# First FFN matrix as seven quarter products, with the residual stream and the inner features passed through DRAM

## The chip, the cores and the metric

The kernel runs on one core of a Trainium2 chip. The metric is the device time of one execution in microseconds. The engines are TensorE (PE; its weight loads are shown as PEld), VectorE (DVE), ScalarE (ACT), GpSimd (POOL) and SyncE (SP), which here only issues DMA. Each engine takes its own instructions in order; semaphores make one wait for another.

## The reference

One step of a decoder layer (depth 1, width 2048) on 512 prompt tokens and 8 sample tokens: modulated norm, one input projection into sliding-window attention and an RWKV-7 mixer, output projection, gated residual; then the FFN, which is what the change touches:

```python
h2 = _modulate(_rmsnorm(x, g_norm_ffn[l]), sh2, sc2)
gate, up = jnp.split(h2 @ w_ffn_in[l], 2, axis=-1)      # 2048 -> 2 x 5632
x = x + gt2[:, None, :] * ((jax.nn.silu(gate) * up) @ w_ffn_out[l])   # 5632 -> 2048
y = _rmsnorm(x, g_norm_final)
```

## The kernel before

Activations are stored feature by partition: 16 blocks of 128 features, and the 520 tokens as two halves of `HB` = 260 columns (256 of the prompt, 4 of the samples). The residual `x1` stays in SBUF from the output projection to the end.

Matrix products run on float32r halves: a value is cast to a high part, and the rest is a low part (`split`, L143 and L144). `unit` (L81) loads 128x512 of a weight by SP into `raw` (3 buffers), ACT casts `wh` (L88), DVE subtracts to `wl` (L91), each with 3 buffers. `mm3` (L94) then issues, for each 128x128 weight block, three products (high by high, high by low, low by high) for each column half. `main_tile` forms one output tile of 128 features: 16 blocks x 3 x 2 = 96 matmuls into two PSUM banks.

`wout_half` ends the output projection one column half after the other, so that half 0 is normed (`norm_half`, a background generator stepped by `pump` with rough costs in `PacedCore`) while half 1 still multiplies. It does this in weight units that serve 12 matmuls. `accumulate` and `accumulate_half` (L1167, L1178) add a PSUM tile, times the gate, to the residual.

`ffn_phase` follows. `first_pair` runs half 0 of the first gate and up tile while half 1 is normed. Then there are 11 blocks of 4 feature tiles: for each feature tile a gate tile and an up tile (`main_tile`), Silu on ACT (L1417), the product on DVE (L1421), the split into `gH`, `gL`. After the first tile of a block, `out_block` multiplies the block before by its rows of the second matrix, 16 output tiles of 24 matmuls, each accumulated in `x1`. `last_block` ends by halves, with the final norm and the writes.

The tile framework fixes each engine's order when the program is built: it takes the instructions by the order of the program, and sets one behind others where its operands or buffers are not free yet by its own reckoning. It adds the semaphores.

## Time and profile before

| | |
|---|---|
| median of 3 runs | 2761.9 us (2759.91 to 2763.59) |
| the profiled execution, its own time | 2761.62 us |
| its span, first to last instruction | 2759.8 us |
| mean granted TensorE clock | 0.982 |
| busy: PE, DVE, ACT, POOL | 2679.3, 1356.5, 923.4, 223.6 us |
| HBM read, written | 332.86 MB, 18.55 MB |

Times are in microseconds from the span's start. In a group of instructions "x352" is the count; then come busy time, mean nanoseconds of one, and the idle time of the engine ahead of them with what ended it. A busy PE is not the same as a PE at its peak, since matmuls overlap: the step from one to the next is read from a stretch of time and the count in it.

### The profile page before, as it was taken

The numbers are of one execution on the slowest core, as the hardware profiler recorded it, in microseconds if no ns is written. First come the engines' busy times: TensorE is split into PE (matmuls) and PEld (weight loads), VectorE is DVE, ScalarE is ACT, GpSimd is POOL, SyncE is SP. The second block draws the span as 40 slices with busy tenths as digits, with TensorE's granted clock in tenths as the row PEclk, the third lists the DMA queues.
The fourth block names the chain that finished last, engine by engine and source line by source line (L and its number), as shares of the span: only waits on it lengthen the run. The fifth ranks groups of instructions, "written<-read, shape, count | busy, mean of one in ns | idle before, by whom it ended". The sixth has DMA issues, their size and how long they took to land.

```text
span 2759.8 us, 58911 instructions
## 1 busy us (share of the span) xinstructions
PE 2679.3 (97%) x24461; PEld 2479.0 (90%) x24461; DVE 1356.5 (49%) x3266; ACT 923.4 (33%) x1816; POOL 223.6 (8%) x300
## 2 busy tenths in 40 slices
PE   7899999999999999989999999999999999999998
PEld 5577777887787898979999999999999999999997
DVE  2465677767755465682434343434343434343436
ACT  3133445455432344552222222222222222222225
POOL 1012122222111000130000000000000000000004
PEclk9899999999989999999999999999999999999999
DMA  8865554555556732322222222222222222222223
GB/s 296 308 200 149 153 152 141 161 150 151 175 163 206 255 133 100 113 80 92 91 93 90 93 92 93 92 92 93 92 93 92 92 93 92 93 92 93 90 96 110
DMA packets 189900, 354.25 MB, mean 128 GB/s; under 512 B 27665, under 2 KB 38849, under 8 KB 189345
## 3 DMA queue, kind: packets, MB, share of 16 engines
q1 hardware_dynamic: 185584, 339.30, 37.1%
q0 software_dynamic: 3408, 10.15, 1.2%
q8 instruction: 191, 3.13, 0.5%
q10 hardware_dynamic: 640, 1.05, 0.1%
q14 instruction: 77, 0.62, 0.1%
HBM read 332.86 MB, written 18.55 MB: 127 GB/s over the span
## 4 chain that ended last, share of the span: by engine, by line
PE 59%; DVE 2%; DMA 1%; ACT 1%; POOL 0%; issue 0%; DVEq 0%; SPq 0%; ACTq 0%; POOLq 0%
PE pm L98 36%; PE pf L98 18%; PE po L98 3%; PE pl L49 1%; PE pO L49 0%; PE pt L49 0%; PE psc L49 0%; DVE wl L91 0%; DVE x L1178 0%; DMA raw<-in_w_fi 0%; DVE h2L L49 0%; DVE u L49 0%; ACT h2H L49 0%; DMA raw<-in_w_out 0%; POOL u L49 0%
## 5 line engine op out<-in xcount | busy, mean ns | idle before, releaser
L88 ACT CAST wh<-raw 128x512 fp32r<-128x512 f32 (+2 forms) x751 | 460.9, 615 | 1266.8 <-PE pm L98 807.1
L91 DVE TENSOR_TENSOR wl<-raw,wh 128x512 fp32r<-128x512 f32 (+2 forms) x751 | 522.3, 697 | 690.2 <-ACT wh L88 688.8
L98 PE MATMUL pm<-h2H,wh 128*128 128x260 f32 x2816 | 571.2, 282 | 2.2 <-ACT wh L88 1.2
L98 PE MATMUL pm<-h2L,wh 128*128 128x260 f32 x2816 | 572.1, 283 | 0.7 <-DVE h2L L49 0.4
L98 PE MATMUL pm<-h2H,wl 128*128 128x260 f32 x2816 | 572.4, 283 | 0.0
L98 PEld LDWEIGHTS pm<-h2H,wh 128*128 128x128 f32 x2816 | 435.9, 188 | 2.9 <-ACT wh L88 1.3
L98 PEld LDWEIGHTS pm<-h2L,wh 128*128 128x128 f32 x2816 | 435.0, 188 | 1.7 <-DVE h2L L49 1.5
L98 PEld LDWEIGHTS pm<-h2H,wl 128*128 128x128 f32 x2816 | 436.3, 188 | 0.0
L98 PE MATMUL pm<-hH,wh 128*128 128x260 f32 (+1 forms) x1248 | 297.6, 318 | 2.8 <-ACT hH L143 1.6
L98 PE MATMUL pf<-gH,wh 128*128 128x260 f32 x1312 | 266.8, 283 | 0.0
L98 PE MATMUL pf<-gH,wl 128*128 128x260 f32 x1312 | 266.4, 282 | 0.0
L98 PE MATMUL pf<-gL,wh 128*128 128x260 f32 x1312 | 266.4, 282 | 0.0
L98 PE MATMUL pm<-hL,wh 128*128 128x260 f32 (+1 forms) x1248 | 264.7, 292 | 0.2 <-DVE hL L144 0.2
L98 PE MATMUL pm<-hH,wl 128*128 128x260 f32 (+1 forms) x1248 | 262.5, 291 | 0.0
L98 PEld LDWEIGHTS pm<-hH,wh 128*128 128x128 f32 (+1 forms) x1248 | 195.9, 192 | 51.8 <-issue 33.1
L1167 DVE SCALAR_TENSOR_TENSOR x<-pf,mod,x 128x512 f32<-128x512 f32 x160 | 120.1, 750 | 215.1 <-PE pf L98 215.1
L98 PEld LDWEIGHTS pf<-gH,wl 128*128 128x128 f32 x1312 | 203.4, 188 | 0.0
L98 PEld LDWEIGHTS pf<-gL,wh 128*128 128x128 f32 x1312 | 203.2, 188 | 0.0
L98 PEld LDWEIGHTS pf<-gH,wh 128*128 128x128 f32 x1312 | 203.2, 188 | 0.0
L98 PEld LDWEIGHTS pm<-hH,wl 128*128 128x128 f32 (+1 forms) x1248 | 197.6, 192 | 6.0 <-issue 1.8
L98 PEld LDWEIGHTS pm<-hL,wh 128*128 128x128 f32 (+1 forms) x1248 | 198.0, 192 | 5.4 <-issue 2.0
L1186 POOL TENSOR_TENSOR acc<-sqh 128x260 f32<-128x260 f32 x4 | 3.0, 742 | 1662.1 <-ACT sqh L1183 1471.3
(372 smaller groups left out, 3100.2 us busy)
## 6 DMA issues: line engine op xcount, KB each, us to landing
raw<-in_w_fi SPq DMA_DIRECT2D x352, 256.0 KB, 2.5
ar<-in_w_ada SPq DMA_DIRECT2D x256, 256.0 KB, 3.1
raw<-in_w_fo SPq DMA_DIRECT2D x176, 256.0 KB, 2.5
raw<-in_w_in SPq DMA_DIRECT2D x148, 256.0 KB, 3.6
araw<-in_w_ada SPq DMA_DIRECT2D x64, 512.0 KB, 6.0
raw<-in_w_out SPq DMA_DIRECT2D x74, 256.0 KB, 2.9
catl<-catd SPq DMA_DIRECT2D x16, 256.0 KB, 2.8
x<-in_x SPq DMA_DIRECT2D x4, 780.0 KB, 7.8
```

The costliest lines, as they stand in the source:

```text
L49: return f(out, *a, **kw)
L88: nc.scalar.copy(wh[:, :n], raw[:, :n])
L91: nc.vector.tensor_tensor(wl[:, :n], raw[:, :n], wh[:, :n].bitcast(F32), ALU.subtract)
L98: nc.tensor.matmul(ps[:m, bank, :HB], w, a[:, k, h, :], start=first and i == 0, stop=last and i == 2, skip_group_check=True,)
L1167: nc.vector.scalar_tensor_tensor(x[:, :, 0:256], ps[:, :, 0:256], self.mod[:, gt + o, 0:1], x[:, :, 0:256], ALU.mult, ALU.add)
L1186: nc.gpsimd.tensor_tensor(acc, sq[:, 0], sq[:, 1], ALU.add)
```

## The change

For each of the 44 feature tiles the first matrix is taken as a 2 x 2 block product (Winograd's form of Strassen's method). The blocks of the weights are A11 (gate, k blocks 0 to 7), A12 (gate, 8 to 15), A21 and A22 (the same of up); those of the activations are B11, B21 (half 0, the two k ranges) and B12, B22 (half 1). Seven products of 8 k blocks on one column half replace eight: A11 B11, A12 B21, (A21+A22) T1, (A21+A22-A11) T2, (A11-A21) T3, A22 T4, (A12-(A21+A22-A11)) B22, with T1 = B12-B11, T2 = B22-T1, T3 = B22-B12, T4 = T2-B21. POOL forms the weight sums, in two steps `g` of 4 k blocks, from four loads of 128x512. Every operand is split into high and low after the sum. DVE adds the products as they leave PSUM.

`norm_first` splits half 0 (`B0`) and keeps its values; `norm_second` forms B22 and T1 to T4. The residual now lies in eight tiles of two blocks each (`x_tiles8`). T3 and T4 take their buffers, so the residual goes to DRAM (`x1d`) as the output projection makes it and comes back in `ffn_out`. The features go to DRAM (`gd`), except for the last four tiles. `ffn_out` multiplies by the second matrix in segments of one or two blocks and fetches the features of the next segment. The first two products of three feature tiles run ahead of the loop, since they need half 0 alone.

```diff
+            self.x1d = [self.dr.tile([P, 2, 2, HB], F32, name=f"x1d{i}") for i in range(8)]
+            self.gd = [self.dr.tile([P, 2, HB], F32, name=f"gd{i}") for i in range(FT)]
...
-                self.x1 = self.xp.tile([P, KD, 2, HB], F32, name="x1")
+                self.x_tiles8()
                 self.start(self.x_load())
...
-                self.fp = st.enter_context(tc.tile_pool(name="fpa", bufs=1, **R))
-                self.h2H = self.fp.tile([P, KD, 2, HB], F32R, name="h2H")
-                self.h2L = self.fp.tile([P, KD, 2, HB], F32R, name="h2L")
+                self.fpa, self.fpb, self.nb = ExitStack(), ExitStack(), 12
+                self.fp = self.fpa.enter_context(tc.tile_pool(name="fpa", bufs=1, **R))
+                self.B0 = [self.fp.tile([P, KD, HB], F32R, name=n) for n in ("B0H", "B0L")]
+                self.xs = self.scat
                 self.make_G(SC2, P_GF)
                 kept = {}
                 with tc.tile_pool(name="wk", bufs=1) as self.wk:
                     self.wout_half(0, kept)
-                    self.start(self.norm_half(0, self.aux))
+                    self.start(self.norm_first(self.aux))
                     self.wout_half(1, kept)
                     self.drain()
-            self.ffn_phase()
+            with tc.tile_pool(name="psf", bufs=4, space=PSUM) as self.ps_m:
+                self.ffn_in(st)
+                self.ffn_out()
...
+    def x_tiles8(self):
+
+        self.x1 = [None] * 8
+        for i in (0, 4, 1, 5, 2, 6, 3, 7):
+            self.x1[i] = self.xp.tile([P, 2, 2, HB], F32, tag="x", bufs=8, name=self.nm("x1"))
...
-        sq = self.fp.tile([P, 2, HB], F32, tag="sqh", bufs=2, name=self.nm("sqh"))[:, 0:n]
+        if gt == GT1:
+            nc.gpsimd.tensor_copy(self.xs[:, o:o + n, h], x[:, :, 256:260])
+            nc.gpsimd.dma_start(self.x1d[o // 2][:, o % 2:o % 2 + n, h], x)
...
+    def norm_start(self, nc, h, r):
+        us = self.fp.tile([P, KD, 4], F32, tag="us", name=self.nm("us"))
+        nc.vector.tensor_tensor(us, self.xs[:, :, h], r[:, sc].unsqueeze(1).broadcast_to([P, KD, 4]), ALU.mult)
+        nc.vector.tensor_tensor(us, us, self.G[:, :, ms], ALU.mult)
+        nc.vector.tensor_tensor(us, us, self.mod[:, SH2:SH2 + KD, ms], ALU.add)
+        return us
+    def norm_pair(self, nc, h, kp, r, us):
+        k = 2 * kp
+        hb = self.fp.tile([P, 2, HB], F32, tag="n", bufs=self.nb, name=self.nm("hb"))
+        nc.vector.tensor_tensor(hb[:, :, 0:256], self.x1[kp][:, :, h, 0:256],
+                                r[:, 0:256].unsqueeze(1).broadcast_to([P, 2, 256]), ALU.mult)
+        nc.gpsimd.tensor_copy(hb[:, :, 256:HB], us[:, k:k + 2])
+        for i in range(2):
+            nc.scalar.activation(hb[:, i, 0:256], hb[:, i, 0:256], AF.Identity, bias=self.mod[:, SH2 + k + i, 0:1],
+                                 scale=self.G[:, k + i, 0:1])
+        return hb
+    def cut(self, nc, H, L, src):
+        nc.scalar.copy(H, src)
+        nc.vector.tensor_tensor(L, src, H.bitcast(F32), ALU.subtract)
+    def norm_first(self, psum):
+        nc = self.px
+        r = self.norm(0, psum("ssq2"), nc)
+        yield
+        us = self.norm_start(nc, 0, r)
+        self.hb0 = []
+        for kp in range(8):
+            hb = self.norm_pair(nc, 0, kp, r, us)
+            self.hb0.append(hb)
+            ks = slice(2 * kp, 2 * kp + 2)
+            self.cut(nc, self.B0[0][:, ks], self.B0[1][:, ks], hb)
+    def norm_second(self, psum):
+        nc = self.nc
+        r = self.norm(1, psum("ssq2"), nc)
+        us = self.norm_start(nc, 1, r)
+        yield
+        sub = ALU.subtract
+        put = lambda f, kp, src: self.cut(nc, f[kp][:, 0], f[kp][:, 1], src)
+        for kp in range(4):
+            b11, b21 = self.hb0[kp], self.hb0[kp + 4]
+            b12 = self.norm_pair(nc, 1, kp, r, us)
+            nc.gpsimd.tensor_tensor(b11, b12, b11, sub)
+            yield
+            b22 = self.norm_pair(nc, 1, kp + 4, r, us)
+            put(self.T1, kp, b11)
+            yield
+            nc.gpsimd.tensor_tensor(b12, b22, b12, sub)
+            put(self.B22, kp, b22)
+            nc.vector.tensor_tensor(b22, b22, b11, sub)
+            yield
+            nc.gpsimd.tensor_tensor(b21, b22, b21, sub)
+            put(self.T2, kp, b22)
+            yield
+            for f, src in ((self.T3, b12), (self.T4, b21)):
+                f.append(self.xp.tile([P, 2, 2, HB], F32R, tag="x", bufs=8, name=self.nm("xT")))
+                put(f, kp, src)
+            yield
+    def ffn_in(self, st):
+        fb = self.fpb.enter_context(tc.tile_pool(name="fpb", bufs=1, side="right"))
+        quads = lambda n: [fb.tile([P, 2, 2, HB], F32R, name=f"{n}_{i}") for i in range(4)]
+        self.B22, self.T1, self.T2 = quads("B22"), quads("T1"), quads("T2")
+        self.T3, self.T4 = [], []
+        plain = lambda k0: lambda k: [a[:, k0 + k] for a in self.B0]
+        quad = lambda f: lambda k: [f[k // 2][:, i, k % 2] for i in range(2)]
+        B11, B21 = plain(0), plain(8)
+        B22, T1, T2, T3, T4 = map(quad, (self.B22, self.T1, self.T2, self.T3, self.T4))
+        sp = self.fpb.enter_context(tc.tile_pool(name="strw", bufs=1))
+        ct = lambda tag, n: sp.tile([P, 2, HB], F32, tag=tag, bufs=n, name=self.nm(tag))
+        src = lambda ht, row, col, g: I["w_fi"][2 * ht + row][:, 1024 * col + 512 * g:1024 * col + 512 * g + 512]
+        def load(ht, row, col, g, tag="sr"):
+            pool, n = (self.w, 3) if tag == "raw" else (sp, 6)
+            t = pool.tile([P, 512], F32, tag=tag, bufs=n, name=self.nm(tag))
+            nc.sync.dma_start(t, src(ht, row, col, g))
+            return t
+        def weights(t):
+            wh, wl = (self.w.tile([P, 512], F32R, tag=n, bufs=3, name=self.nm(n)) for n in ("wh", "wl"))
+            self.cut(nc, wh, wl, t)
+            return wh, wl
+        def product(ps, w, b, g):
+            wh, wl = w
+            for k in range(4):
+                s = slice(k * 128, k * 128 + 128)
+                bH, bL = b(4 * g + k)
+                for i, (x, y) in enumerate(((wh, bH), (wh, bL), (wl, bH))):
+                    nc.tensor.matmul(ps[:, :HB], x[:, s], y, start=g == k == i == 0,
+                                     stop=g == 1 and k == 3 and i == 2, skip_group_check=True)
+        def first_sums(pc, ps):
+            nc.scalar.copy(pc[:, 1], ps[:, 0, :HB])
+            nc.vector.tensor_tensor(pc[:, 0], ps[:, 1, :HB], pc[:, 1], ALU.add)
+        norm = self.norm_second(lambda nm: mt(nm)[:, 0])
+        early = []
+        for ht in range(3):
+            ps = mt("pm")
+            for g in range(2):
+                for col, b in enumerate((B11, B21)):
+                    product(ps[:, col], weights(load(ht, 0, col, g, "raw")), b, g)
+                    next(norm, None)
+            pc = ct("pc", 3)
+            first_sums(pc, ps)
+            early.append(pc)
+        self.kept = []
+        for ht in range(FT):
+            pc = early.pop(0) if early else None
+            old = pc is not None
+            if not old:
+                pc, p12 = ct("pc", 3), mt("pm")
+            p45, p67, p3 = mt("pm"), mt("pm"), mt("pm")
+            for g in range(2):
+                a11, a21 = load(ht, 0, 0, g), load(ht, 1, 0, g)
+                a22 = load(ht, 1, 1, g, "raw")
+                a12 = load(ht, 0, 1, g)
+                s3 = self.w.tile([P, 512], F32, tag="ar", bufs=3, name=self.nm("s3"))
+                nc.gpsimd.tensor_tensor(s3, a11, a21, ALU.subtract)
+                nc.gpsimd.tensor_tensor(a21, a21, a22, ALU.add)
+                if not old:
+                    product(p12[:, 0], weights(a11), B11, g)
+                    w2 = weights(a12)
+                    nc.gpsimd.tensor_tensor(a11, a21, a11, ALU.subtract)
+                    nc.gpsimd.tensor_tensor(a12, a12, a11, ALU.subtract)
+                    product(p12[:, 1], w2, B21, g)
+                    if g == 1:
+                        first_sums(pc, p12)
+                else:
+                    nc.gpsimd.tensor_tensor(a11, a21, a11, ALU.subtract)
+                    nc.gpsimd.tensor_tensor(a12, a12, a11, ALU.subtract)
+                if ht == 0 and g == 0:
+                    for _ in range(12):
+                        next(norm, None)
+                for ps, a, b in ((p45[:, 1], a21, T1), (p67[:, 0], a11, T2), (p67[:, 1], s3, T3),
+                                 (p45[:, 0], a22, T4), (p3[:, 0], a12, B22)):
+                    product(ps, weights(a), b, g)
+                    if ht == 0 and g == 0:
+                        next(norm, None)
+                        next(norm, None)
+                    if g == 0:
+                        continue
+                    if b is T2:
+                        nc.vector.tensor_tensor(pc[:, 1], p67[:, 0, :HB], pc[:, 1], ALU.add)
+                    elif b is T3:
+                        cu = ct("cu", 2)
+                        nc.vector.tensor_tensor(cu[:, 1], p67[:, 1, :HB], pc[:, 1], ALU.add)
+                    elif b is T4:
+                        nc.vector.tensor_tensor(cu[:, 0], cu[:, 1], p45[:, 0, :HB], ALU.subtract)
+                        nc.vector.tensor_tensor(pc[:, 1], p45[:, 1, :HB], pc[:, 1], ALU.add)
+                        nc.vector.tensor_tensor(cu[:, 1], p45[:, 1, :HB], cu[:, 1], ALU.add)
+            nc.vector.tensor_tensor(pc[:, 1], p3[:, 0, :HB], pc[:, 1], ALU.add)
+            nc.scalar.activation(pc, pc, AF.Silu)
+            nc.vector.tensor_tensor(cu, pc, cu, ALU.mult)
+            if ht < FT - 4:
+                nc.gpsimd.dma_start(self.gd[ht], cu)
+            else:
+                gs = [self.fp.tile([P, 2, HB], F32R, tag="n", bufs=self.nb, name=self.nm("g" + c)) for c in "HL"]
+                self.cut(nc, gs[0], gs[1], cu)
+                self.kept.append([a.unsqueeze(1) for a in gs])
+        self.fpb.close()
+    def ffn_out(self):
         with ExitStack() as st:
+            fp = st.enter_context(tc.tile_pool(name="fpo", bufs=1))
+            self.x_tiles8()
+            for i in range(8):
+                nc.gpsimd.dma_start(self.x1[i], self.x1d[i])
+            def part(ps, u, b, gs, first, last, halves=((0, 0), (1, 1))):
+                for n, j in enumerate(gs):
+                    s = slice(j * 128, (j + 1) * 128)
+                    self.mm3(ps, P, u[0][:, s], u[1][:, s], gs[j][0], gs[j][1], 0, first and n == 0,
+                             last and n == len(gs) - 1, halves)
+            def weights(b, o, **kw):
+                return self.unit(I["w_fo"][b, o // 2][:, o % 2 * 512:o % 2 * 512 + 512], **kw)
+            def fetch(ht):
+                raw = fp.tile([P, 2, HB], F32, tag="gr", bufs=2, name=self.nm("gr"))
+                nc.sync.dma_start(raw, self.gd[ht])
+                t = fp.tile([P, 2, 2, HB], F32R, tag="go", bufs=13, name=self.nm("go"))
+                self.cut(nc, t[:, 0], t[:, 1], raw)
+                got.append((t[:, 0:1], t[:, 1:2]))
+            NB = FT // 4
+            got = []
+            gs = dict(enumerate(self.kept))
+            us = [weights(NB - 1, o) for o in range(3)]
+            pss = [mt("pf") for o in range(3)]
+            for js in ((0, 1, 2), (3,)):
+                for o in range(3):
+                    part(pss[o], us[o], NB - 1, {j: gs[j] for j in js}, js[0] == 0, js[0] == 3)
+            segments = [(NB - 1,), (0, 1), (2, 3), (4, 5), (6, 7), (8,), (9,)]
+            for n, bs in enumerate(segments[:-1]):
+                if n:
+                    gs = [dict(enumerate(got[4 * i:4 * i + 4])) for i in range(len(bs))]
+                    del got[:4 * len(bs)]
+                nxt = [4 * b + j for b in segments[n + 1] for j in range(4)]
+                for o in range(KD):
+                    if n == 0 and o > 2:
+                        ps = mt("pf")
+                        part(ps, weights(NB - 1, o), NB - 1, gs, True, True)
+                    elif n == 0:
+                        ps = pss[o]
+                    else:
+                        ps = mt("pf")
+                        for i, b in enumerate(bs):
+                            part(ps, weights(b, o), b, gs[i], i == 0, i == len(bs) - 1)
+                    self.accumulate(o, ps, GT2)
+                    while nxt and (o - 1) * len(nxt) >= 0 and len(nxt) > (KD - 1 - o) / 1.5:
+                        fetch(nxt.pop(0))
+                if n == 0:
+                    self.fpa.close()
+            self.fp, self.nb = st.enter_context(tc.tile_pool(name="fpl", bufs=1, side="right")), 2
+            self.last_block(NB - 2, dict(enumerate(got)))
...
+        for u in range(8):
+            units.append([self.unit(I["w_fo"][b, u][:, v * 512:v * 512 + 512], pool=self.fp, bufs=16) for v in range(2)])
+            part(u, 0, mt("pf"))
...
```

More of the change, by code (lines that the diff above doesn't have):

```diff
@@ new lines, in last_block @@
+        for u in range(8):
+            if u == 1:
+                r = self.norm(0, mt("ssq3")[:, 0], nc)
+            part(u, 1, mt("pf"))
+            if u > 1:
+                result(nc.vector, 0, r, 2 * u - 4, 2)
+        for o in (12, 14):
+            result(nc.gpsimd, 0, r, o, 2)
+        r = self.norm(1, mt("ssq3")[:, 0], nc)
+        for eng, o in ((nc.vector, 0), (nc.gpsimd, 8), (nc.vector, 2), (nc.gpsimd, 10), (nc.vector, 4), (nc.vector, 6),
+                       (nc.gpsimd, 14), (nc.vector, 12)):
+            result(eng, 1, r, o, 2)
```

164 lines of the change are left out of this document (32 added, 132 removed).

## The prediction

> **What bounds the kernel now.** I read the page first: the busy rows, the forty slices, the chain that ended last.
>
> ```profile
> span 2759.8 us, 58911 instructions
> PE 2679.3 (97%) x24461; PEld 2479.0 (90%) x24461; DVE 1356.5 (49%) x3266; ACT 923.4 (33%) x1816; POOL 223.6 (8%) x300
> ...
> PE   7899999999999999989999999999999999999998
> ...
> PEclk9899999999989999999999999999999999999999
> ...
> PE pm L98 36%; PE pf L98 18%; PE po L98 3%; PE pl L49 1%; PE pO L49 0%; PE pt L49 0%; PE psc L49 0%; DVE wl L91 0%; DVE x L1178 0%; DMA raw<-in_w_fi 0%; DVE h2L L49 0%; DVE u L49 0%; ACT h2H L49 0%; DMA raw<-in_w_out 0%; POOL u L49 0%
> ```
>
> TensorE carries the chain, mostly by the FFN's two lines (pm: first matrix, pf: second). Next, stretches: busy times in the FFN and at its start, and the chain there.
>
> ```profile
> core 0: us, PE busy (x) PEld busy (x) DVE busy (x) ACT busy (x) POOL busy (x), PEclk, DMA share, GB/s
> 1200.00:1220.00 20.00, 16.65 (x119) 15.84 (x119) 17.49 (x41) 11.29 (x22) 8.14 (x11) 0.92 0.33 115
> 1220.00:1240.00 20.00, 18.47 (x138) 17.22 (x137) 17.72 (x36) 12.79 (x27) 4.09 (x5) 1.00 0.24 84
> 1474.70:2650.00 1175.30, 1175.30 (x9791) 1175.30 (x9790) 441.35 (x906) 290.60 (x474) 0.00 (x0) 1.00 0.26 92
> ...
> 1241.35 95.39 PE pm L98 x792
> 1336.74 45.88 PE pf L98 x384
> ```
>
> The long stretch holds 9791 matmuls in 1175.30 us, 0.1200 us each, without a gap and at the full granted clock; DVE is busy 38% of it and POOL not at all. An FFN instruction fewer on PE is worth 0.12 us, as long as no other engine becomes the bound. The two rows at 1200 to 1240 show the one place where that has happened: DVE is busy 17.5 of 20 us, POOL works beside it, and PE falls to 16.7.
>
> **The change, part by part.** *Fewer matmuls.* The first matrix took 88 tiles x 16 blocks x 3 products of halves (hh, hl, lh) x 2 column halves = 8448 matmuls. Seven quarter products of 8 blocks need 7 x 8 x 3 = 168 per pair of tiles, times 44 = 7392. Every matmul stays 128x128 on 260 columns; that a weight now serves one column half and not two changes nothing in the rows (the half-width stages keep the same step, and there is one weight load per matmul already). 1056 x 0.12 = **-126.8 us**. The second matrix keeps its 4224 matmuls.
>
> *What the other engines get for it, per pair of tiles.* PE now needs 168 x 0.12 = 20.2 us, before 23.0. Rows that price the rest, groups of the steady stretch and of the stages before:
>
> ```profile
> L91 DVE TENSOR_TENSOR wl<-raw,wh 128x512 fp32r<-128x512 f32 x408 | 280.4, 687 | 479.6 <-ACT wh L88 479.6
> L1421 DVE TENSOR_TENSOR gr<-sg,pm 128x520 f32<-128x520 f32 x33 | 23.0, 696 | 57.9 <-PE pm L98 57.9
> L88 ACT CAST wh<-raw 128x512 fp32r<-128x512 f32 x408 | 253.1, 620 | 873.5 <-PE pm L98 557.0 <-PE pf L98 316.5
> L1417 ACT ACTIVATE sg<-pm 128x520 f32<-128x520 f32 x33 | 19.9, 603 | 0.0
> L1178 DVE SCALAR_TENSOR_TENSOR x<-po,mod,x 128x256 f32<-128x256 f32 x32 | 14.1, 471 | 5.9 <-PE po L98 5.8
> ```
>
> The weight units that are split into wh and wl go from 8 of 24 matmuls to 14 of 12. ACT: 14 x 0.62 + 0.60 + a copy of about 0.3 = 9.6 of 20.2 us, not a bound. DVE: 14 wl, one product of 520 elements, and seven sums that read PSUM (nearest row L1178, 0.47). POOL, idle until now, forms eight sums or differences of 128x512 per pair (four for each half loop). How the two engines get on is what the forecast hangs on. The timeline of the head stage shows it:
>
> ```profile
> 908.60 1.28 POOL L49 TENSOR_TENSOR V<-V,BV 128x512 f32<-128x512 f32 x1 [7.76 <-ACT V L49]
> ...
> 473.96 1.04 POOL L49 TENSOR_TENSOR tC<-pc 128x512 f32<-128x512 f32 x1 [4.83 <-issue]
> 474.26 1.29 DVE L91 TENSOR_TENSOR wl<-raw,wh 128x512 fp32r<-128x512 f32 x1 [0.44 <-ACT wh L88]
> ...
> 217.10 1.04 POOL L49 TENSOR_TENSOR tF<-pc 128x512 f32<-128x512 f32 x1 [6.35 <-ACT SC L435]
> 217.39 0.69 DVE L49 TENSOR_TENSOR BV<-pb,V 128x512 f32<-128x512 f32 x1 [0.26 <-PE pb L49]
> ...
> 531.88 2.92 POOL L49 TENSOR_TENSOR tA<-tB,tA 128x512 f32<-128x512 f32 x1 [0.35 <-DVE tB L49]
> 532.04 0.68 DVE L49 TENSOR_TENSOR tH<-tH,pc 128x512 f32<-128x512 f32 x1
> 532.64 0.68 DVE L91 TENSOR_TENSOR wl<-raw,wh 128x512 fp32r<-128x512 f32 x1
> 533.24 0.41 DVE L49 TENSOR_SCALAR tD<-tD 128x512 f32<-128x512 f32 x1
> ```
>
> A two-input POOL sum of this size takes 1.28 us alone. A wl that meets a running POOL sum ends at 475.55, 0.55 after POOL's end at 475.00: it waited and then took 0.55. A DVE instruction with one input in PSUM (BV<-pb,V) keeps its 0.69 beside POOL. And POOL, when three DVE instructions stand in its way, needs 2.92, of which 1.15 lie after the last of them ended at 533.65; the DVE ones follow each other at 0.60 and lose nothing. So the two exclude each other; whoever is back to back goes on, and PSUM sums are free of it.
>
> The Trainium skill ("SBUF — State Buffer", Who interferes with whom) says the same in general and so speaks against this change: a DVE instruction with two SBUF inputs and a GpSimd one that reads SBUF do not run together, the later one blocks. The rows above agree (1.29 against 0.69). By a reading without that rule the loop would cost nothing; by it, it has the price that follows.
>
> Per pair: DVE's fifteen two-input instructions hold SBUF for 15 x 0.55 = 8.3, POOL's eight for 8 x 1.28 = 10.2, together 18.5 of PE's 20.2 us. The seven PSUM sums, 0.40 each where they follow back to back (0.47 less the overlap of some 0.07 that the 0.60 steps of 0.68 show), add 2.8 on DVE, 21.3 if none falls under a POOL sum. So the loop ends between 20.2 (PE) and 21.3; the far end, all in single file at full durations, is 14 x 0.69 + 0.70 + 10.2 + 7 x 0.47 = 23.8. Half of the sums under POOL gives about 20.8, which I take: 44 x 0.6 = **+26 us** (0 to 50; far end 160).
>
> *The split of the second half's activations.* Before, the norm of half 1 ran beside the first two tiles' work on half 0 and then fed half 1 block by block, and PE hardly waited:
>
> ```profile
> L49 DVE SCALAR_TENSOR_TENSOR h2L<-u,mod,h2H 128x256 fp32r<-128x256 f32 x16 | 8.1, 538 | 0.3 <-ACT h2H L49 0.3
> L49 ACT ACTIVATE h2H<-u,mod 128x256 fp32r<-128x256 f32 x16 | 7.5, 502 | 4.1 <-POOL u L49 3.5 <-DVE u L49 0.6
> L49 DVE RECIPROCAL rstdh<-rstdh 128x260 f32<-128x260 f32 x1 | 1.8, 1769 | 0.0
> ...
> PE pm L98 <- ACT wh L88: 1.2, 1, 1.2
> ```
>
> Now PE has 12 early units and the five of the first half loop before it needs all of it: 17 x 12 x 0.12 = 24.5 us. The five new operands cost twenty splits (DVE 0.60 each), eight scalings (0.60) and four DVE differences (0.60), 19 us, beside 17 wl (10 us), three PSUM sums and the reciprocal: 33 us on DVE. POOL has twelve differences and the first sums of weights, some 22 us. Bounds: DVE alone, with 5 us until the norm is known, 38 - 24.5 = 13; both in single file, 55 - 24.5 = 30. I take 20, between them, since sums and splits here are nearly all two-input: **+20 us**. The pairs before it (half 0's norm under the out projection) trade POOL's five products for copies and stores and DVE's 32 short instructions for 16 long ones: 0, within 3 either way.
>
> *Through DRAM.* Stores are POOL's: some 18 for x, one for each of 40 feature tiles, about 0.6 of issue each; that is 0.6 in POOL's 20 us. Behind a store that waits for its tile stand POOL's sums of the next half loop, which have ten us in hand. Loads come back in the second stage.
>
> ```profile
> GB/s 296 308 200 149 153 152 141 161 150 151 175 163 206 255 133 100 113 80 92 91 93 90 93 92 93 92 92 93 92 93 92 92 93 92 93 92 93 90 96 110
> ...
> x<-in_x SPq DMA_DIRECT2D x4, 780.0 KB, 7.8
> raw<-in_w_fo SPq DMA_DIRECT2D x176, 256.0 KB, 2.5
> L618 POOL DMA_DIRECT2D ABd<-AB x8 | 7.4, 930 | 83.1 <-DVE L L49 83.1
> L49 POOL DMA_DIRECT2D out_wkvs<-sS x4 | 2.4, 588 | 7.7 <-DVE sS L49 5.4 <-DVE Z L49 2.3
> ```
>
> The residual's 4.3 MB come in eight loads of 532 KB, each shorter than the 7.8 us row, started when the operands in their place are done with, half a tile pair before the stage ends; the four PSUM tiles give PE 4 x 24 x 0.12 = 11.5 us before the first sum must have left, and each later load 5.8. The last four tiles' features never leave SBUF, and three output tiles start on three of the four, 6.5 us, over the last sum, Silu, product and split (some 3 us). Feature loads (2.5 us) and splits lie one segment ahead on SP's queue; only the last three of eight wait for a buffer (thirteen), which comes free during the last output tile of 5.8 us. Cost 0; without that cover 14 us for the residual (4.3 MB at the 300 GB/s of the first slices) and 6 at each of five segment ends. I take **+2**. The accumulations fall from 160 to 96, on a DVE that waits anyway: 0. The end (last block, norm, writes) keeps its form: **+1** (-2 to 5).
>
> **Sum:** -126.8 + 26 + 20 + 2 + 1 = -77.8. The profiled execution has a span of 2759.8 and 1.8 around it, 2761.6, as good as the median of 2761.9 (0.01%). 2761.6 - 77.8 = **2684 us**.
>
> **The rivals.** *A, POOL fits in for nothing.* DVE waited in the steady stretch for over half of the time, and POOL's operands are ready a half loop ahead, so that its sums can fall into DVE's waits. Then the loop is PE's 20.2 and the start its lower bound: 2761.6 - 126.8 + 13 + 2 = 2650. Against: 18.5 of 20.2 us of exclusive use leave little to move.
>
> *B, the slower side: DVE and POOL in single file set the loop.* Place: the pair loop; price 23.8 - 20.2 = 3.6, x 44 = 160, with the start at 30: 2761.6 - 126.8 + 160 + 30 + 3 = 2828. It decides from a loop of 22.5 us, where 44 x 2.36 eats the 104 us that the other terms leave. For: 1200 to 1240, where both are loaded and PE gives up a sixth. Against: the 0.60 steps of the 531.88 row; durations overlap, and DVE loses nothing when it has the turn.
>
> *C, DVE's order.* DVE takes its instructions in order, and a sum that waits for a product has the wl of the next units behind it. If a wl stood behind each sum, PE would lose 0.40 + 0.69 - 0.24 = 0.85 at five places per pair; at one place in three 1.7 per pair, 74 us: 2732 (without the +26, with the +23 of the others). Against: the out projection's first half pass has units of 12 matmuls too, with sums of PSUM between their splits and POOL at work, and PE is not short there (stretches, then two of DVE's splits with the sums between):
>
> ```profile
> 1155.00:1160.00 5.00, 5.00 (x44) 5.00 (x43) 3.67 (x12) 2.47 (x4) 0.74 (x1) 1.00 0.57 187
> 1165.00:1170.00 5.00, 5.00 (x44) 5.00 (x43) 5.00 (x12) 2.94 (x5) 3.24 (x4) 1.00 0.51 172
> ...
> 1157.66 0.81 DVE L91 TENSOR_TENSOR wl<-raw,wh 128x512 fp32r<-128x512 f32 x1 [1.30 <-ACT wh L88]
> 1158.39 0.86 DVE L1178 SCALAR_TENSOR_TENSOR x<-po,mod,x 128x256 f32<-128x256 f32 x2
> ```
>
> *D, the passes through DRAM don't hide:* 14 + 30 on top of the forecast, 2728.
>
> **How the numbers follow.** Forecast 0.40, A 0.24, B 0.14, C 0.12, D 0.10. Faster by over 0.2% (5.5 us, about what this measurement tells from no change): forecast and A nearly whole, most of C and D, 0.80; within it 0.04; slower 0.16, B and a worse C. The range runs from a little under A (2640) to over C and D and the upper ends of forecast and start (2770); B lies outside. The forecast's own range is 2660 to 2715.
>
> **What would show it.** In the profile after: 7392 matmuls in the first matrix; a pair every 20.8 us with DVE over 80% busy and wl above its 0.69, POOL sums above 1.28; a gap of about 20 us of PE just after the out projection; no PE gap at the second matrix's start or its segments. It is wrong if PE waits for wl or for POOL's sums by more than 2 us per pair, if wl keeps 0.69 beside POOL, or if PE waits for x or the feature tiles.

## The result, and the profile after

The changed kernel takes 2713.8 us (median; 2710.1 to 2716.8) against 2760.9 us before (2755.6 to 2763.6): a ratio of 0.983 (95% interval 0.981 to 0.985), 47 us less. The forecast was 2684, 78 us less. Its profiled execution took 2716.8 us with a span of 2714.9, so the two spans differ by 44.9 us, and that is the difference accounted for below.

First the page of the changed kernel: span, busy times, the forty slices of four rows, and the chain that ended last.

```profile
span 2714.9 us, 59056 instructions
PE 2586.2 (95%) x23405; PEld 2369.0 (87%) x23405; DVE 1824.8 (67%) x3637; ACT 1109.9 (41%) x2142; POOL 808.4 (30%) x755
...
PE   6899999999999999985999999999999999999997
...
DVE  2466677767756364688888888888888863444457
...
POOL 0012121211212000066655556555655510000004
PEclk9899999999989998997999999999999999999999
...
PE pm L1400 27%; PE pf L98 18%; DVE wl L1244 2%; ACT wh L1243 1%; DVE pc L1463 1%; DVE cu L1460 1%; DVE pc L1461 0%; POOL sr L1435 0%; DMA gr<-gd 0%; POOL sr L1431 0%; DVE x L1546 0%; PE ssq L1214 0%; DVE cu L1462 0%; DVE rstdh L1217 0%; DVEq L1681 0%
```

PE executes 23405 matmuls, 1056 fewer than the 24461 of before, as the change says. PE still carries the chain, but wl, wh and the FFN's sums now appear in it by whole per cents, where before they stood at nothing. Two places stand out in the slices: PE's 5 in the nineteenth (1222 to 1290 us, just after the output projection), with the granted clock at 7, and DVE's 8 and POOL's 5 and 6 through the whole pair loop.

Next, stretches of the changed kernel: the start of the FFN (from the last output-projection matmul to 1300 us), three pieces of it, the start up to the first regular pair, all 41 regular pairs, a steady stretch of 37 of these, and the second matrix. A regular pair is one with all seven products in it; the first three pairs have five, since their first two ran early. The columns are busy time and count for each engine, the mean granted clock, the DMA share and GB/s.

```profile
core 0: us, PE busy (x) PEld busy (x) DVE busy (x) ACT busy (x) POOL busy (x), PEclk, DMA share, GB/s
1218.60:1300.00 81.40, 50.04 (x332) 47.17 (x331) 67.02 (x79) 39.28 (x71) 56.10 (x46) 0.79 0.33 108
1220.00:1240.00 20.00, 11.52 (x81) 10.63 (x82) 15.71 (x21) 10.08 (x20) 12.12 (x15) 0.85 0.54 172
1240.00:1260.00 20.00, 11.18 (x70) 10.32 (x70) 16.91 (x20) 11.96 (x24) 16.34 (x12) 0.76 0.23 79
1260.00:1280.00 20.00, 9.42 (x50) 8.89 (x50) 18.17 (x17) 8.71 (x16) 14.83 (x10) 0.62 0.13 40
1218.60:1323.80 105.20, 72.54 (x513) 69.17 (x512) 87.93 (x104) 49.19 (x87) 72.48 (x58) 0.84 0.35 116
1323.80:2189.86 866.06, 851.51 (x6890) 836.36 (x6889) 724.03 (x908) 390.25 (x659) 503.00 (x370) 1.00 0.34 113
1389.50:2170.90 781.40, 768.48 (x6216) 754.78 (x6216) 655.93 (x818) 351.88 (x595) 455.70 (x331) 1.00 0.34 113
2189.90:2699.10 509.20, 506.68 (x4232) 506.09 (x4230) 252.01 (x579) 156.02 (x264) 22.47 (x27) 1.00 0.38 119
```

The same first stretch in the kernel before:

```profile
1214.70:1300.00 85.30, 82.39 (x665) 80.69 (x664) 40.40 (x73) 33.23 (x61) 5.22 (x6) 1.00 0.27 93
```

From these rows comes the account. Let the *excess* of a stretch be its length less 0.12006 us for each FFN matmul in it, which is about the step of the steady stretch before (1175.30 us for 9791). Nine of the counted 332 and 665 belong to the norm and the output projection. In the start the excess by 1300 us is 81.4 - 323 x 0.12006 = 42.6 us after the change and 6.5 before. The first regular pair begins at 1323.8, with an excess of 105.2 - 504 x 0.12006 = 44.7. The 41 regular pairs take 866.06 us for 6888 matmuls, an excess of 39.1: 21.12 us per pair against 20.17 of matmuls. (The 37 pairs of 781.4 us give the same 21.12.) The second matrix adds 2.0. Before, the whole FFN had 8.0. The last output-projection matmul came at 1218.6 against 1214.7, and the tail after the last FFN matmul is 0.2 longer. So -126.8 + (44.7 + 39.1 + 2.0 - 8.0) + 3.9 + 0.2 = -44.9, the measured difference of the spans.

**The loop.** Groups of the 37 pairs in the changed kernel: busy time and mean ns of one, then the idle time before and what ended it.

```profile
L1244 DVE TENSOR_TENSOR wl<-sr,wh 128x512 fp32r<-128x512 f32 x372 | 411.2, 1121 | 85.3 <-ACT wh L1243 70.3 <-PE pm L1400 1.8
L1400 PEld LDWEIGHTS pm<-B0H,wl 128*128 128x128 f32 x592 | 111.6, 189 | 18.1 <-DVE wl L1244 17.6
L1244 DVE TENSOR_TENSOR wl<-raw,wh 128x512 fp32r<-128x512 f32 x74 | 50.6, 684 | 0.5
L1436 POOL TENSOR_TENSOR sr<-sr,sr 128x512 f32<-128x512 f32 x74 | 118.5, 1601 | 28.7 <-POOL sr L1435 25.8
L1435 POOL TENSOR_TENSOR sr<-sr,sr 128x512 f32<-128x512 f32 x74 | 112.3, 1517 | 18.2 <-DVE wl L1244 18.2
L1430 POOL TENSOR_TENSOR s<-sr,sr 128x512 f32<-128x512 f32 x74 | 95.9, 1296 | 241.6 <-DMA sr<-in_w_fi 198.5 <-DVE wl L1244 43.1
L1465 DVE TENSOR_TENSOR cu<-pc,cu 128x520 f32<-128x520 f32 x37 | 66.2, 1790 | 0.0
L1458 DVE TENSOR_TENSOR cu<-pm,pc 128x260 f32<-128x260 f32 x37 | 15.9, 429 | 35.7 <-PE pm L1400 35.7
```

Of DVE's instructions with two SBUF inputs, most are stretched: ten wl of each pair from 0.69 to a mean of 1.12 us, the product from 0.70 to 1.79. The other four wl (two from raw, shown, and two from s) keep 0.68. Of POOL's four sums in a half loop the first keeps 1.30 for its 1.28, and the rows shown of the others take 1.5 and 1.6. The sums that read PSUM keep 0.43. DVE is at 655.93/781.4 = 84%. The weight loads of PE wait for wl.

**The start.** PE's waits between 1218.6 and 1300 (us in total, times, longest), then pieces of the timelines of PE, ACT, DVE and POOL there (start, duration, idle before).

```profile
PE pm L1400 <- DVE wl L1244: 15.8, 7, 8.5
PE pm L1400 <- ACT wh L1243: 14.4, 2, 8.0
```

```profile
1237.11 0.59 PE L1400 MATMUL pm<-B0H,wh 128*128 128x260 f32 x1 [6.47 <-ACT wh L1243]
...
1240.77 0.42 PE L1400 MATMUL pm<-B0H,wh 128*128 128x260 f32 x1
1240.99 0.42 PE L1400 MATMUL pm<-B0L,wh 128*128 128x260 f32 x1
...
1235.91 0.63 ACT L1243 CAST xT<-hb 128x520 fp32r<-128x520 f32 x1 [1.63 <-POOL hb L1278]
1236.44 0.61 ACT L1243 CAST wh<-raw 128x512 fp32r<-128x512 f32 x1
...
1234.14 1.73 POOL L1278 TENSOR_TENSOR hb<-hb,hb 128x520 f32<-128x520 f32 x1
...
1247.94 3.93 POOL L1273 TENSOR_TENSOR hb<-hb,hb 128x520 f32<-128x520 f32 x1 [3.58 <-ACT hb L1238]
...
1266.23 1.73 POOL L1282 TENSOR_TENSOR hb<-hb,hb 128x520 f32<-128x520 f32 x1
1267.99 0.63 ACT L1243 CAST xT<-hb 128x520 fp32r<-128x520 f32 x1 [5.55 <-POOL hb L1282]
1268.65 0.70 DVE L1244 TENSOR_TENSOR xT<-hb,xT 128x520 fp32r<-128x520 f32 x1 [1.83 <-ACT xT L1243]
1269.27 0.68 DVE L1244 TENSOR_TENSOR wl<-sr,wh 128x512 fp32r<-128x512 f32 x1
1270.01 0.59 PE L1400 MATMUL pm<-T,wl 128*128 128x260 f32 x1 [8.50 <-DVE wl L1244]
```

PE stands still for 6.47 us until a weight cast (wh) that ACT issues behind an activation cast (xT), which itself waits for a difference on POOL. The longest wait, 8.50 us, has the same chain with one link more: POOL's difference (L1282), ACT's cast of xT, DVE's split of xT, and behind it on DVE the wl for which PE waits. When PE comes back, its matmuls follow each other at 0.22 us instead of 0.12; the granted clock of these stretches is 0.85, 0.76 and 0.62. In the whole start, 73 steps of 0.17 to 0.30 us cost some 7 us of excess and the longer gaps some 37, so most of it is waiting.

**The entry to the second matrix.** ACT and PE there, in the changed kernel:

```profile
2198.62 0.62 ACT L1243 CAST go<-gr 128x520 fp32r<-128x520 f32 x1 [5.66 <-DMA gr<-gd]
...
2200.48 1.66 ACT L88 CAST wh<-raw 128x512 fp32r<-128x512 f32 x3
...
2201.15 0.51 PE L98 MATMUL pf<-gH,wh 128*128 128x260 f32 x2 [2.48 <-ACT wh L88]
```

In the second matrix the DRAM pass shows as one PE gap, 2.48 us up to 2201.15: the weight casts (L88) stand on ACT behind casts of feature tiles that wait for their load.

### The profile page after: what moved, and what is told of

Read it like the earlier page. It is cut to its first block, busy times and chain, and to the rows that moved or that the text cites. A ratio compares the mean times of both kernels' runs of the same rounds, so it can differ in the third digit from the quotient of the medians.

```text
span 2714.9 us, 59056 instructions
## 1 busy us (share of the span) xinstructions
PE 2586.2 (95%) x23405; PEld 2369.0 (87%) x23405; DVE 1824.8 (67%) x3637; ACT 1109.9 (41%) x2142; POOL 808.4 (30%) x755
## 4 chain that ended last, share of the span: by engine, by line
PE 45%; DVE 4%; issue 2%; ACT 1%; POOL 1%; DMA 0%; DVEq 0%; SPq 0%; POOLq 0%; ACTq 0%
PE pm L1400 27%; PE pf L98 18%; DVE wl L1244 2%; ACT wh L1243 1%; DVE pc L1463 1%; DVE cu L1460 1%; DVE pc L1461 0%; POOL sr L1435 0%; DMA gr<-gd 0%; POOL sr L1431 0%; DVE x L1546 0%; PE ssq L1214 0%; DVE cu L1462 0%; DVE rstdh L1217 0%; DVEq L1681 0%
## 5 line engine op out<-in xcount | busy, mean ns | idle before, releaser
L1244 DVE TENSOR_TENSOR wl<-sr,wh 128x512 fp32r<-128x512 f32 x428 | 471.1, 1115 | 99.9 <-ACT wh L1243 83.1
L88 ACT CAST wh<-raw 128x512 fp32r<-128x512 f32 (+2 forms) x411 | 250.0, 611 | 496.7 <-PE pf L98 281.0
L1243 ACT CAST wh<-sr 128x512 fp32r<-128x512 f32 x428 | 265.2, 620 | 365.8 <-PE pm L1400 272.1
L98 PE MATMUL pf<-go,wh 128*128 128x260 f32 x2560 | 414.2, 282 | 0.0
L91 DVE TENSOR_TENSOR wl<-raw,wh 128x512 fp32r<-128x512 f32 (+2 forms) x411 | 287.6, 702 | 177.6 <-ACT wh L88 170.9
L98 PEld LDWEIGHTS pf<-go,wh 128*128 128x128 f32 x2560 | 353.9, 188 | 0.1
L1400 PE MATMUL pm<-T,wh 128*128 128x260 f32 x1408 | 263.3, 285 | 8.0 <-ACT wh L1243 8.0
L98 PE MATMUL pf<-go,wl 128*128 128x260 f32 x1280 | 267.9, 282 | 0.0
L1400 PE MATMUL pm<-xT,wh 128*128 128x260 f32 x1408 | 261.7, 286 | 0.0
L1400 PEld LDWEIGHTS pm<-T,wh 128*128 128x128 f32 x1408 | 219.9, 191 | 8.4 <-ACT wh L1243 8.4
L1400 PEld LDWEIGHTS pm<-xT,wh 128*128 128x128 f32 x1408 | 217.1, 189 | 3.9
L1400 PE MATMUL pm<-T,wl 128*128 128x260 f32 x704 | 203.5, 289 | 12.6 <-DVE wl L1244 12.6
```

Source lines behind the costliest of these rows:

```text
L88: nc.scalar.copy(wh[:, :n], raw[:, :n])
L91: nc.vector.tensor_tensor(wl[:, :n], raw[:, :n], wh[:, :n].bitcast(F32), ALU.subtract)
L98: nc.tensor.matmul(ps[:m, bank, :HB], w, a[:, k, h, :], start=first and i == 0, stop=last and i == 2, skip_group_check=True,)
L1243: nc.scalar.copy(H, src)
L1244: nc.vector.tensor_tensor(L, src, H.bitcast(F32), ALU.subtract)
L1400: nc.tensor.matmul(ps[:, :HB], x[:, s], y, start=g == k == i == 0, stop=g == 1 and k == 3 and i == 2, skip_group_check=True)
```

## The experiments

All are edits of the changed kernel and are compared through their ratio to the kernel before, run beside them on the same chip; their chips differ, so that ratios compare them better than times. "Step" is the mean time of the regular pairs; "start" the excess by 1300 us, counted as above (after: step 21.12, start 42.6). A few expectations count the excess to about 1390 us; by 1389.5 it is 48.2 after the change. Step and start are each read from one profiled execution.

**The sums of weights left out.** POOL's six-line block of weight sums goes; one product takes another operand.

```diff
-                nc.gpsimd.tensor_tensor(s3, a11, a21, ALU.subtract)
-                nc.gpsimd.tensor_tensor(a21, a21, a22, ALU.add)
 (and the two differences in both branches)
-  (p67[:, 1], s3, T3)
+  (p67[:, 1], a22, T3)
```

> The changed kernel without POOL's weight sums: the products take the loaded blocks themselves (the operand of T3 is A22), so what is left out is the sums of weights, and the first matrix is not the reference's. All matmuls, splits, PSUM sums and transfers stay. Theory (DVE and POOL exclude each other at SBUF): the step from pair to pair falls from 21.1 to 20.2-20.3 us, the wl splits go back to 0.69 us, the product of gate and up from 1.7 to 0.7; with some 5 us at the start that is 2670 to 2680 us. Rival (a sum of PSUM that waits for its product holds up the splits behind it, whatever POOL does): the step stays at 21 us, 2705 to 2715.

Measured: 2674.3 us, ratio 0.970 (0.967 to 0.972); step 20.37, start 28.3. The total is where the theory had it. The last 37 pairs in this kernel, and their groups of wl and of the product:

```profile
1391.70:2145.20 753.50, 753.50 (x6218) 748.37 (x6217) 470.68 (x818) 355.58 (x595) 22.61 (x42) 1.00 0.36 118
...
L1244 DVE TENSOR_TENSOR wl<-sr,wh 128x512 fp32r<-128x512 f32 x369 | 251.6, 690 | 144.6 <-ACT wh L1243 137.0
L1457 DVE TENSOR_TENSOR cu<-pc,cu 128x520 f32<-128x520 f32 x37 | 25.7, 693 | 0.0
```

Without POOL at work wl is back at 0.690 and the product at 0.693, and the step falls by 0.75. So POOL's sums beside DVE's splits cost the loop 44 x 0.75 = 33 us at most (with the sums goes also the wait for their results), and some 14 of the start. What DVE's order alone costs (rival C) can be no more than the 20.37 - 20.17 that is left. That rest is taken up below.

**The sums of weights on DVE.**

```diff
-                nc.gpsimd.tensor_tensor(s3, a11, a21, ALU.subtract)
+                nc.vector.tensor_tensor(s3, a11, a21, ALU.subtract)
 (and so the other five)
```

> All eight weight sums per pair move from POOL to DVE, nothing else. Theory (exclusion): a sum costs DVE 0.60 us back to back and nobody is blocked any more, so DVE has 11.8 + 4.8 = 16.6 us of work in PE's 20.2, and the step falls to 20.2-20.5: 2675 to 2690 us. Rival (DVE is just full, its order decides): 4.8 us more on DVE per pair lengthen the step to 22 us or more, 2740 to 2760.

Measured: 2725.9 us, ratio 0.988 (0.984 to 0.991); step 21.63, start 32.4. This missed both expectations: 12 us slower than the change, not faster, and not by as much as the rival had it. PE's waits in the loop of this kernel:

```profile
PE pm L1400 <- DVE pc L1455: 16.0, 28, 1.8
PE pm L1400 <- DVE wl L1244: 6.4, 33, 0.9
```

wl took 0.69 again, but PE now waits for L1455. That is DVE's sum which reads the second product (T2) from one half of a two-bank PSUM tile, p67[:, 0]; the next product (T3) writes the other half, p67[:, 1], and is held until the read is done. With six more sums ahead of it on DVE the read comes late. The next experiment asks whether the change, with an emptier DVE queue, has the same hold.

**Other pairs in the PSUM tiles.** Only the places of the products change, so that one which follows at once lies in another tile.

```diff
-  (p45[:, 1], a21, T1), (p67[:, 0], a11, T2), (p67[:, 1], s3, T3), (p45[:, 0], a22, T4), (p3[:, 0], a12, B22)
+  (p45[:, 1], a21, T1), (p45[:, 0], a11, T2), (p67[:, 0], s3, T3), (p3[:, 0], a22, T4), (p67[:, 1], a12, B22)
 (the sums read the places accordingly)
```

> The new pairing of PSUM tiles alone, all sums on POOL. If the shared tile costs the changed kernel something too (PE's short steps ahead of T3 and T4, some 0.14 us per pair), 5 to 10 us less, 2704 to 2709; if only the exclusion counts, 2711 to 2717.

Measured: 2706.0 us, ratio 0.980 (0.978 to 0.981); step 20.92, start 40.1. So 0.20 us of each pair, some 9 us of the loop, went with the places of the products, and not with POOL's sums. It is the 0.20 that the first experiment left over. There it can be seen in T3's second half loop: DVE's sum (L1447) reads T2's half of the tile, and PE's four steps beside it take 0.68 us instead of 0.48. The last row is from the kernel with other places, where such steps stay at 0.12.

```profile
1672.46 0.43 DVE L1447 TENSOR_TENSOR pc<-pm,pc 128x260 f32<-128x260 f32 x1 [0.23 <-PE pm L1400]
1672.61 0.84 PE L1400 MATMUL pm<-xT,wh 128*128 128x260 f32 x4
1673.29 0.28 PE L1400 MATMUL pm<-xT,wl 128*128 128x260 f32 x1
...
1692.56 0.40 PE L1400 MATMUL pm<-xT,wh 128*128 128x260 f32 x2
```

**Both: sums of weights on DVE, and other pairs.**

> All weight sums on DVE as in the second run, and the PSUM tiles paired anew: T1 with T2, T3 with B22, T4 alone, so that no product is followed by one into the other bank of its own tile. Theory (that run lost its time in T3's second step, which waited for DVE to read T2's bank of the same tile): the step falls from 21.6 to 20.4-20.7 us, 2680 to 2695. Rival (DVE in order is too full for PE at 16.6 us of 20.2): stays at 21.3 or more, 2712 to 2728.

Measured: 2685.2 us, ratio 0.971 (0.968 to 0.974); step 20.46, start 33.0. A stretch of the loop, PE's waits in it, and the groups of wl and of one of the sums:

```profile
1389.50:2146.20 756.70, 750.22 (x6210) 746.18 (x6210) 631.57 (x1111) 356.91 (x595) 20.53 (x38) 1.00 0.36 116
...
PE pm L1400 <- DVE cu L1458: 6.1, 10, 1.3
PE pm L1400 <- DVE wl L1244: 0.2, 1, 0.2
...
L1244 DVE TENSOR_TENSOR wl<-sr,wh 128x512 fp32r<-128x512 f32 x370 | 252.8, 684 | 39.4 <-ACT wh L1243 38.7
L1435 DVE TENSOR_TENSOR sr<-sr,sr 128x512 f32<-128x512 f32 x74 | 50.7, 685 | 1.3
```

The same edit that lost 12 us with the old places gains 21 with the new ones (2706.0 to 2685.2 on this chip), so the loss of the second experiment was the shared tile. DVE now does 23 instructions with two SBUF inputs a pair, at 0.69, and is 83% busy, about as much as beside POOL (84%), but PE hardly waits for wl.

**Half of the sums on each engine, other pairs.** a11 and a12 on DVE, s3 and a21 on POOL.

> The new pairing, with two of the four sums of a half loop (A21+A22-A11 and the last one) on DVE and the other two on POOL. Theory (exclusion): 15 x 0.55 + 4 x 0.55 + 4 x 1.28 = 15.6 us of exclusive use against 18.5, DVE 14.2 us; the step falls to 20.4-20.7, 2685 to 2697 us. Rival (any POOL sum blocks the product of gate and up and the split behind it as before): 20.9 or more, 2702 to 2714.

Measured: 2703.7 us, ratio 0.978 (0.977 to 0.980); step 20.78, start 36.9. The total met the rival's range, and the step lies between the two, nearer to all on POOL (20.92) than to all on DVE (20.46): half of POOL's sums still costs 0.32 of the 0.46.

**The differences of activations on DVE** (twelve, at the start; the weights' sums stay on POOL).

```diff
-            nc.gpsimd.tensor_tensor(b11, b12, b11, sub)
+            nc.vector.tensor_tensor(b11, b12, b11, sub)
 (and so the two others)
```

> Only the twelve differences of activations at the start move from POOL to DVE; the loop is untouched. Theory (at the start too, DVE and POOL stand in each other's way): 7 us more on DVE against 20 us less on POOL, so the excess between the output projection and the steady loop (48 us) falls by 10 to 20: 2695 to 2705 us. Rival (the start is held by the order in which ACT and DVE take splits and weights, not by POOL): within 4 us of the changed kernel or slower, 2711 to 2722.

Measured: 2715.9 us, ratio 0.984 (0.981 to 0.987); step 21.21, start 36.8. The total met the rival, and the fall of the start, 6 us by 1300 and 7 by 1389.5, is short of the 10 to 20 that the theory had. The total shows nothing of it (the last output-projection matmul came at 1221.2, 2.6 later, and the step is 0.09 longer). It can't carry a verdict on this edit; the start speaks for a small gain.

**Five early tiles instead of three**, so that PE has more work that needs nothing of half 1.

```diff
-        for ht in range(3):
+        for ht in range(5):
-            pc = ct("pc", 3)
+            pc = ct("pc", 5)
-                        cu = ct("cu", 2)
+                        cu = ct("cu", 1)
 (and one activation buffer fewer, to make room)
```

> Five feature tiles instead of three run their first two products ahead of the loop (the buffers for it from one of the two cu and one of the twelve n), nothing else: 8 more units, 11.5 us of PE work that needs half 0 alone. Theory (the start lacks PE work to cover the splits): the excess of 48 us between the output projection and the steady loop falls by 7 to 11, 2703 to 2708 us. Rival (the weights of those products stand behind the splits on ACT and DVE, so PE waits whatever work there is): 2710 to 2718.

Measured: 2711.9 us, ratio 0.981 (0.979 to 0.983); step 21.17, start 34.0. This gave no clear answer. The total is 2 us under the change, as the rival had it, but by the ratios it is 7 under, with intervals that overlap. The start is 9 us shorter by 1300 and by 1389.5, as the theory had it, but the profiled execution is the fastest of the four (2701.7, the others 2711.9 to 2714.4), and its last output-projection matmul came 9 us earlier than in the change. The edit also takes a cu buffer and an activation buffer away. The last experiment but one asks again.

**Eight plain products**: the new structure (DRAM passes, second matrix apart, half-width tiles), without Strassen's sums.

> The new structure (residual and features through DRAM, second matrix as its own stage, half 1 in the residual's buffers) with the eight plain products instead of the seven: 192 matmuls per pair, no sums of weights or activations. Theory (the passes through DRAM are nearly free, 3 to 5 us): 2755 to 2772 us, about the kernel before, with a step of 23.05 us. Rival (the passes cost tens of us, and the seven products gain more than it seems): 2785 or more.

Measured: 2771.7 us, ratio 1.004 (1.001 to 1.006); step 23.08. Its loop:

```profile
1381.70:2235.90 854.20, 854.20 (x7108) 854.20 (x7107) 229.91 (x337) 229.93 (x412) 18.38 (x34) 1.00 0.30 101
```

PE has no gap in it at all. The structure costs 12.6 us against the kernel before it ran beside (2759.1; by the ratio 10), more than the 3 to 5 expected: the last output-projection matmul comes 5.8 later, the FFN's excess is 16.4 against 8.0 (10.0 of it in the start, 5.0 in the second matrix). The seven products then gain 2771.7 - 2713.8 = 58 us (by the ratios, 0.0204 x 2761 = 56) of the 126.8 that fewer matmuls are worth.

**All sums on DVE, other pairs.** Sums of weights on DVE and other pairs as above (the sixth run), and the twelve differences on DVE too.

> The sixth run (weight sums on DVE, new pairing of PSUM tiles) with the twelve activation differences on DVE too, so that POOL has no sum beside DVE in the FFN. Its excess between the output projection and about 1390 us is 34 us now. Theory (POOL's differences block DVE there, splits of 1.8 and 2.4 us): 24 to 28, total 2674 to 2681 us. Rival (the number of splits and their order hold it): 32 or more, 2682 to 2690.

Measured: 2677.5 us, ratio 0.969 (0.967 to 0.971); step 20.48, start 26.6. Its total is where the theory had it; its excess by 1389.5, 29.1 us against 33.8 in the sixth run, fell a little less than the 24 to 28 expected. With the next kernel, which is level with it, it is the fastest that computes everything, 36 us under the change (39 by the ratios) and 87 under the kernel before.

**The same with five early tiles.**

> The run before with five early feature tiles instead of three. If PE lacks work that needs half 0 alone, once nothing blocks DVE, another 6 to 10 us less than that run: 2665 to 2674. If the weights of these products stand behind the splits, within 4 us of it.

Measured: 2676.7 us, ratio 0.968 (0.966 to 0.970); step 20.55, start 24.2. On the same chip as the kernel without the two tiles, the total is level, and by the first regular pair so is the excess (27.6 against 27.3). So once DVE has all the sums, more work that needs half 0 alone gains nothing: PE did not lack products to do. It lacked their weights, which are split by the same two engines, in one order with the activations, as the two chains above show.

**The differences of activations left out**, with the sums of weights on DVE and other pairs.

```diff
-            nc.gpsimd.tensor_tensor(b11, b12, b11, sub)
-            nc.gpsimd.tensor_tensor(b12, b22, b12, sub)
-            nc.vector.tensor_tensor(b22, b22, b11, sub)
-            nc.gpsimd.tensor_tensor(b21, b22, b21, sub)
```

> The sixth run without any difference of activations: T1 to T4 are splits of the plain values, so the sums of activations are left out, and the first matrix is not the reference's; all twenty splits and eight scalings stay. If the sums cost the start most of its 34 us, the excess falls to 15 or less, 2665 or less; if the splits and their order do, it stays at 20 to 28, 2672 to 2680.

Measured: 2667.5 us, ratio 0.965 (0.962 to 0.968); step 20.52, start 15.9. The start of the last kernel but two, and of this one:

```profile
1224.50:1300.00 75.50, 57.09 (x416) 53.97 (x415) 72.26 (x127) 44.01 (x79) 8.06 (x15) 0.89 0.43 138
```

```profile
1227.40:1300.00 72.60, 63.13 (x481) 60.67 (x480) 67.22 (x118) 44.66 (x82) 7.86 (x18) 0.95 0.49 161
```

This fell between the expectations: the excess by 1389.5 is 19.4 us where the sixth run has 33.8, the total 2.5 us above the lower one's bound. With DVE's sums of weights in both, leaving the differences out takes 33.0 - 15.9 = 17.1 us off the start, moving them to DVE 6.4. DVE is busy for 96% and 93% of these two stretches, which suggests that it bounds the start with and without them; no run shows that by itself.

## Why the prediction was right and wrong

*The terms of the sum, forecast and measured* (us against the kernel before):

| step | forecast | measured |
|---|---|---|
| fewer matmuls | -126.8 | -126.8 (1056 x 0.12006) |
| pair loop, over PE's time | +26 | +39 (41 regular pairs) |
| start: split of half 1 | +20 | +37 (44.7 - 8.0) |
| through DRAM | +2 | +2.0 |
| stage before | 0 | +3.9 |
| end | +1 | +0.2 |
| sum | -78 | -45 |

The forecast's loop is for all 44 pairs; the three that had their first products early are in the start here. With 0.95 for these too the loop would be 42 and the start 34. By either count both terms were too small: of the 33 us missing, some 13 to 16 are the loop's, 14 to 17 the start's, and 4 the stage before.

- *Fewer matmuls: right.* 7392 in the first matrix, 0.12 each where PE doesn't wait; the plain version's loop without any gap (854.20 us for 7108) confirms the price.
- *The loop: mechanism right, size off by half.* Most wl above 0.69, POOL sums above 1.28 (three of four), DVE above 80% and untouched PSUM sums are all there, and taking POOL's sums away removes the stretching. The step was 21.12 where 20.8 was forecast, inside the bounds of 20.2 and 21.3; that is 0.95 over PE's time for 0.6. Of the missing 0.35, 0.20 is something the working did not have: a product held until DVE has read the other half of its PSUM tile. With other places for the products the step is 20.92, and the working's 20.8 is nearly met. Here the trace also agrees with what the prediction cited from the Trainium skill ("SBUF — State Buffer", Who interferes with whom), that a DVE instruction with two SBUF inputs and a GpSimd one that reads SBUF don't run together: 1.79 against 0.69 for the product, with POOL working and without.
- *The start: the step that failed, mis-sized by nearly half.* The prediction set 33 us of DVE work against 24.5 us of PE work and took 20, between 13 and 30. It measured 37, or 34 with the loop's share taken out, above the bound for single file. The cover was not there: the working let 17 PE units run beside the splits, but ACT and DVE take the splits of activations and of those units' weights in one order, so when an activation's split waits for POOL, the weights wait too, and PE with them (6.47 us behind the wh cast, 8.50 behind a wl). The runs hold this up: more PE work changed nothing once DVE had all the sums (in the changed kernel itself that test stayed open), fewer things in DVE's and POOL's way did shorten the start (by 1300, POOL's weight sums out or on DVE: 28.3 and 32.4 for 42.6; differences on DVE: 36.8; both on DVE, with other places: 26.6; differences out as well: 15.9). On top, PE's clock fell in the gaps, which was not priced; the slow steps cost some 7 us.
- *Through DRAM: right in size.* One gap of 2.5 us, at the second matrix's start, where the prediction had none; none at the segments.
- *The stage before: not to be judged from one execution.* It is 3.9 us, 5.8 in the plain version, just over the 3 that were allowed. But among the edits of the changed kernel the last output-projection matmul lies anywhere from 1209.6 to 1227.4, and what sets it stays open.
- *The rivals.* A fell: POOL's sums are not hidden, and with them out the step is 0.75 shorter. B fell: the step stays under 22.5, from where the change would lose. C fell as it was put: with POOL's sums out, DVE's order leaves at most 0.2 a pair. (Its price was added up wrong: 0.85 at five places, one time in three, is 1.4 a pair, not 1.7, and 62 us, not 74.) But its relative, PE waiting for DVE's *read* of a product, is real, 0.20 a pair here and the loss when DVE got the sums too. D fell.

Still open: how the remaining 16 us of the start (plain version: 10) divide between the order of splits on ACT and DVE and their number. A kernel with weight splits ahead of activation splits was not tried.

## What to carry to other kernels

Where DVE does two-input work most of the time, the idle POOL is no free place for two-input sums: here the same sums on DVE at 0.69 were 21 us cheaper than on POOL (2685.2 against 2706.0), although DVE then had 23 such instructions a pair. That only showed once adjacent products no longer shared a PSUM tile, so look at what a new wait names before giving up an edit. At a handover between stages, don't set the sum of one engine's work against another's: follow the order in each queue, and ask whether the work that is to cover a step needs the same engines first.

## What the runs showed of the hardware that was not expected

- *PE's clock inside a busy kernel.* After the gap of 6.47 us the matmul step is 0.22 us instead of 0.12, and the stretch 1260 to 1280 has a mean granted clock of 0.62. The Trainium skill ("TensorE: Matmul & The Clock Gate", Part 1: The HAM clock gate) says that the clock halves after an idle window of about 3.4 us and returns after about as long a busy one; the fall agrees with the 6.47 us gap and the 0.22 steps, and after a further gap they were back at 0.12 by 1244.6, 4.9 us after PE had taken up work again at 1239.74. The prediction counted a gap only by its length.
- *How far POOL's sums stretch among DVE's.* A difference of 128x520 on POOL took 3.93 us at 1247.94, where 128x512 takes 1.28 alone; in the loop the mean was 1.5 to 1.6 for three of the four sums of a half loop. The stretching is mutual: DVE's product, next to POOL's sum, took 1.79 for 0.69 in nearly every pair (mean of 37).
- *Half the sums on POOL cost more than half.* Two of four per half loop left on POOL kept 0.32 of the 0.46 us per pair that all four cost.
